# Attention scores from two fp32r products a head on stacked high and low parts, and in-chunk products over whole chunks

## The chip, the cores and the metric

The kernel runs on one core of one Trainium2 chip. The metric is the device time of one execution in microseconds. One execution was also profiled; its rows give the start and length of each instruction on five engines: PE (TensorE, the matrix engine; PEld are its weight loads), DVE (VectorE), ACT (ScalarE), POOL (GpSimd) and SP (SyncE, here only an issuer of transfers).

## The reference, cut to what matters

Two layers over 512 tokens of width 1024. The first mixes with a convolution and an RWKV-7 recurrence, the second with sliding-window attention; each is followed by a gated feed-forward block. The change touches two places: the products inside a chunk of the recurrence, which the kernel solves in chunks of 64 tokens, and the attention scores.

```python
def rwkv7_recurrence(r, w, k, v, a, b):
    def step(s, inp):
        r_t, w_t, k_t, v_t, a_t, b_t = inp
        sa = jnp.einsum('bhij,bhj->bhi', s, a_t)
        s = s * w_t[:, :, None, :] + sa[..., None] * b_t[:, :, None, :] + v_t[..., None] * k_t[:, :, None, :]
        return s, jnp.einsum('bhij,bhj->bhi', s, r_t)
...
    q = partial_rope(rms_norm(q, q_norm_g), positions)   # 16 heads of 64
    k = partial_rope(rms_norm(k, k_norm_g), positions)   # 4 heads of 64
...
    # blocks of 128 queries, each against its own and the block before
    s = jnp.einsum('bnqhgd,bnkhd->bnhgqk', q, kc).astype(jnp.float32) * (HEAD_DIM ** -0.5)
```

## The kernel before, in words

Activations lie with channels on the 128 partitions and the 512 tokens along the free dimension. Every large product goes through `gemm` (line 174): weights are loaded in pieces of 512 KB by SP, split into a high fp32r part on ACT (line 150) and a low remainder on DVE (line 151), and three fp32r matmuls of 128 rows and 512 columns (high by high, high by low, low by high) are added up in a PSUM bank. A tile framework orders the instructions of each engine ahead of time, by priorities and its own estimates; each engine then runs its list strictly in that order, and semaphores make it wait. Matmuls of `gemm` are therefore set between the small steps of the other work as filler, but at fixed places.

**In-chunk products** (`keys`, line 413). For each of four groups of channels (two heads each), each of 8 chunks and each head (`eo`), two products of 64 rows by 64 output rows by 128 columns in fp32 are formed, one for each half `d` of the output rows. They take the four 64 by 64 quarters of PE in turn. Four PSUM banks a group come from a ring of three, and DVE masks each bank into `mt` (line 415). The matmul of line 430 and, from the next group, that of line 372 follow.

**Attention.** `queries(j)` makes two query heads: a `gemm` of 24 matmuls, bias and gain on ACT (line 902), sums of squares on PE (line 900), and the rotation `rope`: POOL issues four small transfers that swap rows into `zr` (line 838), DVE multiplies by the signed sine (line 839), multiplies by the cosine and adds (lines 840, 841) into `qr`. Keys go through the same with a PE permutation (line 832) and are copied by eight POOL transfers into `kd`, which holds each of the four key heads twice, on partitions 0 to 63 and 64 to 127. `block(m, b)` then works on the four query heads of key head `m` and query block `b`: four fp32 matmuls on 64 rows give the scores (line 934; head `e` of a pair uses rows `e*64` on), DVE scales, masks and takes the row limit (line 939), ACT exponentiates (line 101), DVE normalizes (line 949), PE transposes (line 953), ACT copies (line 955), PE multiplies by the values on 64 output columns (line 960), and the result is split into `oh` and `ol` on ACT and DVE for the output `gemm`. In block 0 of a head only 128 keys are used, else 256. The loop calls `queries` for the next key head at `b` 0 and 2.

The forms in the profile's rows give the shape in which PE is used, rows by columns: 128\*128 for `gemm`, 64\*128 for the scores, 128\*64 for the product with the values, 128\*32 for the sums of squares, 64\*64 for the in-chunk products.

Of the kernel before, what the change touches and what calls it, by code (L numbers as in the profile page):

```python
# [11 lines left out]
F32 = mybir.dt.float32  # L12
F32R = mybir.dt.float32r
I32 = mybir.dt.int32
AF = mybir.ActivationFunctionType
ALU = mybir.AluOpType
# [3 lines left out]
P = 128  # L20
T = 512
# [8 lines left out]
L = 64  # L30
NCH = T // L
# [5 lines left out]
NKV = 4  # L37
HD = 64
# [7 lines left out]
T3 = 5  # L46
# [22 lines left out]
class Net:  # L69
# [186 lines left out]
    def mixer(self):  # L256
        nc, tc, ap = self.nc, self.tc, self.ap
        V, S, G = nc.vector, nc.scalar, nc.gpsimd
# [5 lines left out]
        with ExitStack() as es:  # L264
            pool = lambda **k: es.enter_context(tc.tile_pool(**k))
            self.banks(es, "m", "s", m=3, s=3, n=2)
            cst = pool(name="mxc", bufs=1)
            big = pool(name="mxb", bufs=1)
            tr = pool(name="mxt", bufs=2)
# [38 lines left out]
            msk = cst.tile([P, 1, P], F32, name="msk")  # L308
            G.memset(msk, 1.0)
            for h in range(2):  # L310
                hp = slice(h * L, (h + 1) * L)
# [52 lines left out]
            def keys(fc):  # L364
# [26 lines left out]
                bk = bks[fc] = t4([P, NCH, P], "bk")  # L391
                ar = tr.tile([P, NCH, P], F32, tag="ar", name="ar")
# [12 lines left out]
                mt = mts[g][:, i]  # L405

                for c0 in range(0, NCH, 4):
                    p4s = [self.psum().rearrange("p (c t) -> p c t", t=P) for _ in range(2)]
                    for c in range(4):
                        for d in range(2):  # L410
                            for eo in range(2):
                                hp, dp = slice(eo * 64, eo * 64 + 64), slice(d * L, (d + 1) * L)
                                nc.tensor.matmul(p4s[eo][dp, c, :], lhsT=bk[hp, c0 + c, dp], rhs=ar[hp, c0 + c, :], start=True, stop=True)
                    for eo in range(2):
                        V.tensor_tensor(out=mt[:, eo, c0 : c0 + 4, :], in0=p4s[eo], in1=msk.to_broadcast([P, 4, P]), op=ALU.mult)
                for d in range(2):
# [390 lines left out]
    def attention(self):  # L807
# [10 lines left out]
        with ExitStack() as es:  # L818
# [9 lines left out]
            def rope(dst, z, j=None):  # L828
                t = tq("rp")
                if j is None:  # L830
                    pp = self.bank("d")
                    nc.tensor.matmul(pp, lhsT=self.perm, rhs=z, start=True, stop=True)
                    V.tensor_tensor(out=t, in0=pp, in1=sin, op=ALU.mult)
                else:
                    pp = zr[j % 2]
                    for o in (0, 8, HD, HD + 8):
                        i = o ^ 8
                        G.dma_start(pp[o : o + 8, :], z[i : i + 8, :])
                    V.tensor_tensor(out=t, in0=pp, in1=self.sgs, op=ALU.mult)
                V.tensor_tensor(out=dst, in0=z, in1=cos, op=ALU.mult)  # L840
                V.tensor_tensor(out=dst, in0=dst, in1=t, op=ALU.add)


            kd = [cst.tile([P, T], F32, name=f"kd{m}") for m in range(NKV)]
            pk = self.gemm(wq, 8, xh, xl)
# [10 lines left out]
            for i in range(2):  # L856
                t = tq("zt")
                V.tensor_tensor(out=t, in0=pk[i], in1=rstd, op=ALU.mult)
                S.activation(out=t, in_=t, func=AF.Identity, bias=self.pc("attn_b_qkv", 8 + i))
                sq = tq("zs")  # L860
                S.activation(out=sq, in_=t, func=AF.Square)
                pss = self.bank("d")
                nc.tensor.matmul(pss, lhsT=self.bdv, rhs=sq, start=True, stop=True)
                rs = self.rsqrt_rows(tr, "t2", pss, 1e-6, "kr", ln=True)
                V.scalar_tensor_tensor(out=t, in0=t, scalar=self.pc("attn_k_norm_g"), in1=rs, op0=ALU.mult, op1=ALU.mult)
                kr = tq("kr")
                rope(kr, t)
                for e in range(2):
                    for o in range(2):
                        G.dma_start(kd[2 * i + e][o * HD : (o + 1) * HD, :], kr[e * HD : (e + 1) * HD, :])  # L870

# [14 lines left out]

            qr = cst.tile([P, 8, T], F32, name="qr")
            rq = cst.tile([P, NB, NH], F32, name="rq")

            def queries(j):  # L890
# [14 lines left out]
                V.tensor_scalar(out=ms, in0=pss, scalar1=1.0 / HD, scalar2=1e-6, op0=ALU.mult, op1=ALU.add)  # L905
                rope(qr[:, j, :], t, j)
                y0 = tr.tile([P, NB, 2], F32, tag="my", name="my")
# [6 lines left out]

            cst.tile([P, 112], F32, name="gap")
            oh = cst.tile([P, DC, T], F32R, name="oh")
            ol = cst.tile([P, DC, T], F32R, name="ol")

            def block(m, b):
# [10 lines left out]
                for hp in range(2):  # L930
                    for e in range(2):
                        h = 4 * m + 2 * hp + e
                        hs = slice(e * HD, (e + 1) * HD)
                        nc.tensor.matmul(pscs[e][:, hp, :nk], lhsT=qr[hs, h // 2, bs], rhs=kd[m][hs, k0 : k0 + nk], start=True, stop=True)  # L934
                for hp in range(2):
# [30 lines left out]
            for m in range(NKV):  # L966
                for b in range(NB):
                    if m < NKV - 1 and b % 2 == 0:
                        queries(2 * m + 2 + b // 2)
                    block(m, b)  # L970
# [77 lines left out]
```

## Time and profile before

| | us |
|---|---|
| median of 3 runs (lowest, highest) | 1225.57 (1220.81, 1232.14) |
| the profiled execution | 1226.35 |
| its span, first to last instruction | 1224.5 |
| PE busy in the span | 1202.0 |
| DVE, ACT, POOL busy in the span | 723.1, 553.0, 71.8 |

The span and what lies around it (1.85 us) make up the profiled execution's time. Busy PE time counts matmuls from start to modelled end, which overlap, so the step from one start to the next tells more than the mean length. Each fp32 matmul of the program is two instructions in the profile, except the transposes; an fp32r matmul is one.

### The profile page before, as it was taken

How to read it: one execution, taken by the hardware profiler on the slowest of the kernel's cores; microseconds unless marked ns; L12 is line 12 of the kernel's file. 1: busy time of each engine (PE TensorE's matmuls, PEld its weight loads, DVE VectorE, ACT ScalarE, POOL GpSimd, SP SyncE). 2: the span in 40 equal slices, each digit the busy share in tenths (PEclk: the TensorE clock that was granted, in tenths of full speed). 3: DMA queues.
4: the chain of work that ended last, by engine and by line, in shares of the span. 5: the costliest groups of instructions: out<-in, count | busy, mean ns of one | idle time of the engine just before them, and what ended most of it. 6: DMA issues, size and time to landing. Idle time of an engine off the chain costs nothing.

```text
span 1224.5 us, 17211 instructions
## 1 busy us (share of the span) xinstructions
PE 1202.0 (98%) x6547; PEld 945.2 (77%) x6547; DVE 723.1 (59%) x1366; ACT 553.0 (45%) x1035; POOL 71.8 (6%) x209
## 2 busy tenths in 40 slices
PE   7999999999999999999999999999999999999998
PEld 5677866568788888888888866668888888888886
DVE  6787974476767555553333778876655555553332
ACT  6877332375544434343222556774544344442221
POOL 4101031000100000000000031100000000000000
PEclk9999996999999999999999999999999999999999
DMA  5144391023322323223333231112223232233331
GB/s 190 50 115 117 94 219 34 2 70 104 99 90 100 104 86 104 98 91 96 98 103 100 87 93 56 42 36 86 88 101 102 87 104 95 95 104 103 120 113 60
DMA packets 65089, 114.45 MB, mean 93 GB/s; under 512 B 15680, under 2 KB 17936, under 8 KB 65008
## 3 DMA queue, kind: packets, MB, share of 16 engines
q1 hardware_dynamic: 60048, 102.25, 26.7%
q0 software_dynamic: 4816, 10.89, 3.6%
q8 instruction: 51, 0.84, 0.3%
q14 instruction: 30, 0.25, 0.1%
q10 hardware_dynamic: 144, 0.23, 0.1%
HBM read 105.40 MB, written 4.26 MB: 90 GB/s over the span
## 4 chain that ended last, share of the span: by engine, by line
PE 89%; DVE 6%; ACT 2%; issue 1%; DMA 1%; POOL 0%; ACTq 0%; DVEq 0%
PE mm L174 63%; PE bank L174 10%; PE mm L636 2%; PE bank L934 2%; PE bank L960 1%; PE bank L953 1%; DVE wlo L151 1%; PE ps L546 1%; PE ps L559 1%; PE ps L565 1%; DVE tb L494 1%; DVE etmp L492 1%; PE ps L530 1%; PE ps L523 1%; PE ps L573 1%
## 5 line engine op out<-in xcount | busy, mean ns | idle before, releaser
L151 DVE TENSOR_TENSOR wlo<-wraw,whi 128x512 fp32r<-128x512 f32 x364 | 250.7, 690 | 349.9 <-ACT whi L150 349.5
L150 ACT CAST whi<-wraw 128x512 fp32r<-128x512 f32 x364 | 225.1, 619 | 419.1 <-PE mm L174 380.5
L174 PE MATMUL mm<-xgh,whi 128*128 128x512 f32 x896 | 352.0, 393 | 9.3 <-ACT whi L150 7.8
L174 PE MATMUL mm<-xgl,whi 128*128 128x512 f32 x896 | 351.3, 392 | 0.0
L174 PE MATMUL mm<-xgh,wlo 128*128 128x512 f32 x896 | 350.8, 392 | 0.0
L174 PEld LDWEIGHTS mm<-xgh,whi 128*128 128x128 f32 x896 | 168.9, 189 | 46.0 <-ACT whi L150 9.2
L174 PEld LDWEIGHTS mm<-xgh,wlo 128*128 128x128 f32 x896 | 168.8, 188 | 38.1 <-issue 2.4
L174 PEld LDWEIGHTS mm<-xgl,whi 128*128 128x128 f32 x896 | 169.0, 189 | 36.3 <-issue 1.7
L174 PE MATMUL mm<-hh,wlo 128*128 128x512 f32 x352 | 137.0, 389 | 0.0
L174 PE MATMUL mm<-hh,whi 128*128 128x512 f32 x352 | 137.0, 389 | 0.0
L174 PE MATMUL mm<-hl,whi 128*128 128x512 f32 x352 | 137.0, 389 | 0.0
L174 PEld LDWEIGHTS mm<-hl,whi 128*128 128x128 f32 x352 | 66.1, 188 | 13.7
L174 PEld LDWEIGHTS mm<-hh,wlo 128*128 128x128 f32 x352 | 66.1, 188 | 13.7
L174 PEld LDWEIGHTS mm<-hh,whi 128*128 128x128 f32 x352 | 66.1, 188 | 13.7
L723 DVE SCALAR_TENSOR_TENSOR t<-gp,col,t 128x512 f32<-128x512 f32 x88 | 63.5, 745 | 0.0
L720 ACT ACTIVATE t<-gp,col 128x512 f32<-128x512 f32 x44 | 35.7, 816 | 35.3 <-DVE gp L718 34.7
L183 ACT CAST hh<-t 128x512 fp32r<-128x512 f32 x44 | 27.2, 621 | 37.0 <-DVE t L726 36.8
L718 DVE TENSOR_TENSOR gp<-mm,rstd 128x512 f32<-128x512 f32 x44 | 30.2, 691 | 17.3 <-PE mm L174 17.2
L726 DVE TENSOR_TENSOR t<-t,mm 128x512 f32<-128x512 f32 x44 | 30.0, 687 | 17.2 <-PE mm L174 17.2
L101 ACT ACTIVATE t<-t 128x512 f32<-128x512 f32 x44 | 27.7, 629 | 20.4 <-DVE t L723 20.3
L717 POOL MEMSET gp<- 128x2 f32 x44 | 4.4, 103 | 506.3 <-DVE t L723 451.0
L939 DVE CUSTOM_DVE_ANT_0 pr<-bank,mask,nsnk 128x256 f32<-128x256 f32 (+1 forms) x64 | 31.4, 503 | 2.0 <-PE bank L934 2.0
(328 smaller groups left out, 1442.8 us busy)
## 6 DMA issues: line engine op xcount, KB each, us to landing
wraw<-in_w_up_dram SPq DMA_DIRECT2D x88, 512.0 KB, 3.4
wraw<-in_w_down_dram SPq DMA_DIRECT2D x40, 512.0 KB, 3.6
wraw<-in_w_in_dram SPq DMA_DIRECT2D x22, 512.0 KB, 3.6
wraw<-in_w_qkv_dram SPq DMA_DIRECT2D x12, 512.0 KB, 3.4
wraw<-in_w_out_dram SPq DMA_DIRECT2D x8, 512.0 KB, 3.6
wraw<-in_w_o_dram SPq DMA_DIRECT2D x8, 512.0 KB, 3.4
st<-cpad POOLq DMA_DIRECT2D x24, 135.0 KB, 4.1
xT<-in_xT_dram SPq DMA_DIRECT2D x4, 512.0 KB, 7.9
```

The source lines that it names most:

```text
L101: ins = self.nc.scalar.activation(**kw)
L150: nc.scalar.copy(hi, src)
L151: nc.vector.tensor_tensor(out=lo, in0=src, in1=hi.bitcast(F32), op=ALU.subtract)
L174: mm = lambda a, b, **kw: self.nc.tensor.matmul(ps, lhsT=a[:, i, k, :], rhs=b[:, kk, :], **kw)
L183: nc.scalar.copy(hi, src)
L636: nc.tensor.matmul(pc[b * 32 : b * 32 + 32, :], lhsT=dg[:, b, g, :], rhs=stk[b][:, 4 * g : 4 * g + T], start=g == 0, stop=g == 7, tile_pos ...
L718: V.tensor_tensor(out=gp[:, 2:], in0=pg[i], in1=rstd, op=ALU.mult)
L720: S.activation(out=t, in_=gp[:, 2:], func=AF.Identity, scale=self.pc("ffn_conv_w", (3 * l + 2) * FC + f), bias=self.pc("ffn_conv_b", l * F ...
L723: V.scalar_tensor_tensor(out=t, in0=gp[:, j : j + T], scalar=self.pc("ffn_conv_w", (3 * l + j) * FC + f), in1=t, op0=ALU.mult, op1=ALU.add)
L726: V.tensor_tensor(out=t, in0=t, in1=pu[i], op=ALU.mult)
L934: nc.tensor.matmul(pscs[e][:, hp, :nk], lhsT=qr[hs, h // 2, bs], rhs=kd[m][hs, k0 : k0 + nk], start=True, stop=True)
L939: V.tensor_tensor_reduce(out=pr_[:, i, :nk], in0=pscs[e][:, hp, :nk], in1=mask[:, 2 * P - nk :], op0=ALU.add, op1=ALU.min, scale=rq[:, b, ...
```

## The change: what it does

In the recurrence, one product of 64 rows by 128 output rows by 128 columns takes the place of two, and the loop over the heads `eo` becomes the outer one: all 8 chunks of one head, then all of the other.

In attention, rotated queries and keys are split into a high fp32r part and a low remainder, each with a cast on ACT and a subtraction on DVE (`split`, lines 183 and 184). Keys: `kd` becomes 128 x 2 x 512, with the high part (index 0) and the low part (index 1) side by side, both on partitions 0 to 63 and again on 64 to 127. Queries: POOL transfers put, for head `e` of a pair, the high part on partitions `e*64` on and the low part on the other 64. The scores of a head are then two fp32r matmuls added up in the same bank: index 0 on all 128 rows (high and low queries by high keys), index 1 on the 64 rows of the high queries (by low keys). Both always run over 256 keys. The sine product of the queries' `rope` moves from DVE to POOL, its tiles move to the ring `t2`, `queries` are called at `b` 0 and 1, and 32 more POOL transfers are issued.

```diff
-                for c0 in range(0, NCH, 4):
-                    p4s = [self.psum().rearrange("p (c t) -> p c t", t=P) for _ in range(2)]
-                    for c in range(4):
-                        for d in range(2):
-                            for eo in range(2):
-                                hp, dp = slice(eo * 64, eo * 64 + 64), slice(d * L, (d + 1) * L)
-                                nc.tensor.matmul(p4s[eo][dp, c, :], lhsT=bk[hp, c0 + c, dp], rhs=ar[hp, c0 + c, :], start=True, stop=True)
-                    for eo in range(2):
-                        V.tensor_tensor(out=mt[:, eo, c0 : c0 + 4, :], in0=p4s[eo], in1=msk.to_broadcast([P, 4, P]), op=ALU.mult)
+                for eo in range(2):
+                    hp = slice(eo * 64, eo * 64 + 64)
+                    for c0 in range(0, NCH, 4):
+                        p4 = self.psum().rearrange("p (c t) -> p c t", t=P)
+                        for c in range(4):
+                            nc.tensor.matmul(p4[:, c, :], lhsT=bk[hp, c0 + c, :], rhs=ar[hp, c0 + c, :], start=True, stop=True)
+                        V.tensor_tensor(out=mt[:, eo, c0 : c0 + 4, :], in0=p4, in1=msk.to_broadcast([P, 4, P]), op=ALU.mult)
...
-                    V.tensor_tensor(out=t, in0=pp, in1=self.sgs, op=ALU.mult)
+                    G.tensor_tensor(out=t, in0=pp, in1=self.sgs, op=ALU.mult)
...
-            kd = [cst.tile([P, T], F32, name=f"kd{m}") for m in range(NKV)]
+            kd = [cst.tile([P, 2, T], F32R, name=f"kd{m}") for m in range(NKV)]
+            pair = lambda n: tr.tile([P, 2, 2, T], F32R, tag="qs", name=n, bufs=2)
+            ks = pair("ks")
...
+                self.split(ks[:, i, 0, :], ks[:, i, 1, :], kr)
                 for e in range(2):
                     for o in range(2):
-                        G.dma_start(kd[2 * i + e][o * HD : (o + 1) * HD, :], kr[e * HD : (e + 1) * HD, :])
+                        G.dma_start(kd[2 * i + e][o * HD : (o + 1) * HD], ks[e * HD : (e + 1) * HD, i])
...
-                rope(qr[:, j, :], t, j)
+                qr = t2("qr")
+                rope(qr, t, j)
+
+                if j % 2 == 0:
+                    qs[j // 2] = pair("qs")
+                q = [tr.tile([P, T], F32R, tag="t2", name=n, bufs=T3) for n in ("qh", "ql")]
+                self.split(q[0], q[1], qr)
+                for e in range(2):
+                    for d in range(2):
+                        G.dma_start(qs[j // 2][d * HD : (d + 1) * HD, j % 2, e, :], q[d ^ e][e * HD : (e + 1) * HD, :])
...
                 for hp in range(2):
-                    for e in range(2):
-                        h = 4 * m + 2 * hp + e
-                        hs = slice(e * HD, (e + 1) * HD)
-                        nc.tensor.matmul(pscs[e][:, hp, :nk], lhsT=qr[hs, h // 2, bs], rhs=kd[m][hs, k0 : k0 + nk], start=True, stop=True)
+                    for j in range(2):
+                        for e in range(2):
+                            hs = slice(e * HD, (e + 1) * HD) if j else slice(0, P)
+                            nc.tensor.matmul(pscs[e][:, hp, :], lhsT=qs[m][hs, hp, e, bs], rhs=kd[m][hs, j, k0 : k0 + 2 * P], start=j == 0, stop=j == 1)
...
-                    if m < NKV - 1 and b % 2 == 0:
-                        queries(2 * m + 2 + b // 2)
+                    if m < NKV - 1 and b < 2:
+                        queries(2 * m + 2 + b)
```

The order of PE's matmuls moves with it, at three places. The rows below are those of the built programs; one row may stand for several equal matmuls in a row (x4), numbers behind a name tell buffers apart, and L944, L963, L970 and L411 are the new lines of scores, transposes, products with the values and in-chunk products.

First, PE in the attention of the last key head (kd3), before:

```order
L953 MATMUL bank_7049<-ident_66,pr_7026 128x128 x4
L934 MATMUL bank_7110<-kd3_5653,qr_5955 128x256 x2
L953 MATMUL bank_7055<-ident_66,pr_7026 128x128 x4
L960 MATMUL bank_7061<-pT_7023,vt_5830 64x256 x2
L934 MATMUL bank_7154<-kd3_5653,qr_5955 128x256 x2
L960 MATMUL bank_7061<-pT_7023,vt_5830 64x256 x2
L934 MATMUL bank_7155<-kd3_5653,qr_5955 128x256 x2
L934 MATMUL bank_7199<-kd3_5653,qr_5955 128x256 x2
```

Now:

```order
L944 MATMUL bank_7227<-kd3_5590,qs_6846 128x256 x4
L174 MATMUL bank_7321<-ol_5900,whi_7359 128x512
L174 MATMUL bank_7321<-oh_5899,wlo_7360 128x512
L174 MATMUL bank_7321<-oh_5899,whi_7359 128x512
L174 MATMUL bank_7321<-ol_5900,whi_7359 128x512
L174 MATMUL bank_7321<-oh_5899,wlo_7360 128x512
L174 MATMUL bank_7322<-ol_5900,whi_7359 128x512
L944 MATMUL bank_7228<-kd3_5590,qs_6846 128x256 x4
L174 MATMUL bank_7322<-oh_5899,wlo_7360 128x512
L944 MATMUL bank_7276<-kd3_5590,qs_6846 128x256 x4
```

Two matmuls on 64 rows filled a bank's two heads before; now four do, for each of the two heads one on 128 rows and then one on 64, so the shape changes from one matmul to the next. Counted along the whole order from the first key rotation (line 832, now 829) to the end, PE's shape changes 101 times before and 176 times now; 136 of the 176 have a score matmul on one side or both (79 on both), against 58 before. From the first score matmul to the last product with the values stand 157 matmuls of `gemm` before and 120 now; the other 37 moved ahead of the first score.

Second, PE at the in-chunk products of the first group of channels, before:

```order
L174 MATMUL mm<-xgh,whi 128x512
L174 MATMUL mm<-xgl,whi 128x512
L413 MATMUL ps<-ar,bk 64x128 x24
L430 MATMUL bank<-rk,bd_191 128x512
L413 MATMUL ps<-ar,bk 64x128 x8
L372 MATMUL bank<-ku,bdh 128x512
L174 MATMUL mm<-xgh,wlo 128x512
```

Now:

```order
L174 MATMUL mm<-xgh,whi 128x512
L174 MATMUL mm<-xgl,whi 128x512
L411 MATMUL ps<-ar,bk 128x128 x16
L427 MATMUL bank<-rk,bd_191 128x512
L372 MATMUL bank<-ku,bdh 128x512
L174 MATMUL mm<-xgh,wlo 128x512
```

The second visit to the products behind line 430 is gone; the 16 wide ones stand together, 8 on the lower 64 rows and then 8 on the upper 64.

Third, PE at the end of attention, from the last transposes but one block on, before:

```order
L953 MATMUL bank<-ident,pr 128x128 x4
L174 MATMUL bank<-oh,whi 128x512
L174 MATMUL bank<-ol,whi 128x512
L960 MATMUL bank<-pT,vt 64x256 x2
L174 MATMUL bank<-oh,wlo 128x512
L960 MATMUL bank<-pT,vt 64x256 x2
L174 MATMUL bank<-oh,whi 128x512
L174 MATMUL bank<-ol,whi 128x512
L174 MATMUL bank<-oh,wlo 128x512
```

Now, from the last score matmuls on:

```order
L944 MATMUL bank<-kd_5590,qs 128x256 x3
L963 MATMUL bank<-ident,pr 128x128 x8
L970 MATMUL bank<-pT,vt 64x256 x4
L963 MATMUL bank<-ident,pr 128x128 x8
L970 MATMUL bank<-pT,vt 64x256 x4
L963 MATMUL bank<-ident,pr 128x128 x8
L970 MATMUL bank<-pT,vt 64x256 x4
L174 MATMUL bank<-oh,whi 128x512
```

The matmuls of the output `gemm` that stood between transposes and products with the values have moved ahead; none stands behind the last score until the last product.

## Rows read from the trace of the kernel before

**Rows 1.** The page: each engine's busy time.

```profile
PE 1202.0 (98%) x6547; PEld 945.2 (77%) x6547; DVE 723.1 (59%) x1366; ACT 553.0 (45%) x1035; POOL 71.8 (6%) x209
```

**Rows 2.** PE's waits, 690 to 835 us: for whom, total us, times, longest.

```profile
PE bank L953 <- DVE pr L949: 0.8, 2, 0.5
PE bank L960 <- ACT pT L955: 0.2, 1, 0.2
```

**Rows 3.** Two stretches: us, busy PE, PEld, DVE, ACT, POOL, clock, DMA, GB/s.

```profile
745.00:770.00 25.00, 25.00 (x196) 16.17 (x194) 21.28 (x83) 18.53 (x56) 4.01 (x8) 1.00 0.22 69
800.90:824.10 23.20, 22.82 (x135) 13.55 (x134) 17.56 (x75) 18.16 (x55) 0.00 (x0) 1.00 0.08 24
```

**Rows 4.** PE in order of time (start, us): fp32r on two shapes in turn.

```profile
32.81 0.39 PE L174 MATMUL mm<-xgh,wlo 128*128 128x512 f32 x1
33.04 0.39 PE L174 MATMUL mm<-xgh,whi 128*128 128x512 f32 x1
33.36 0.50 PE L359 MATMUL bank<-lis,lws 64*128 64x512 f32 x2
33.79 0.51 PE L174 MATMUL mm<-xgl,whi 128*128 128x512 f32 x1
34.22 0.73 PE L359 MATMUL bank<-lis,lws 64*128 64x512 f32 x4
```

**Rows 5.** PE in order of time: scores, last transposes, `gemm` again.

```profile
722.88 0.39 PE L174 MATMUL bank<-xgh,whi 128*128 128x512 f32 x1
723.40 0.92 PE L934 MATMUL bank<-kd,qr 64*128 64x128 f32 x6
...
747.07 1.13 PE L934 MATMUL bank<-kd,qr 64*128 64x256 f32 x4
748.13 1.09 PE L953 MATMUL bank<-ident,pr 128*128 128x128 f32 x8
748.98 0.47 PE L174 MATMUL bank<-xgh,wlo 128*128 128x512 f32 x1
...
812.03 1.13 PE L934 MATMUL bank<-kd,qr 64*128 64x256 f32 x4
...
821.30 0.27 PE L953 MATMUL bank<-ident,pr 128*128 128x128 f32 x1
...
824.11 0.50 PE L174 MATMUL bank<-oh,whi 128*128 128x512 f32 x1
```

**Rows 6.** PE in order of time: fp32r matmuls of 256 columns, one after the other.

```profile
701.63 0.28 PE L879 MATMUL mm<-wlo,xgh 128*128 128x256 f32 x1
701.75 0.28 PE L879 MATMUL mm<-whi,xgl 128*128 128x256 f32 x1
```

**Rows 7.** PE in order of time, without `gemm`: in-chunk products of the second group.

```profile
73.75 1.97 PE L413 MATMUL ps<-ar,bk 64*64 64x128 f32 x48 [0.15 <-DVE bk L395]
75.65 1.13 PE L430 MATMUL bank<-rk,bd 128*128 128x512 f32 x2
76.78 1.09 PE L413 MATMUL ps<-ar,bk 64*64 64x128 f32 x16
77.80 1.12 PE L372 MATMUL bank<-ku,bdh 128*128 128x512 f32 x2
```

**Rows 8.** POOL: two row swaps, landing times of `kd`, a selection, a fill.

```profile
716.31 1.02 POOL L838 DMA_DIRECT2D zr<-zt  x2
DMA to landing us min/median/max: 2.2/2.8/5.8
L313 POOL TENSOR_SCALAR_AFFINE_SELECT msk<-msk 64x64 f32<-64x64 f32 x4 | 2.6, 663 | 0.1
L826 POOL MEMSET zr<- 128x512 f32 x2 | 1.0, 528 | 148.3 <-DVE t L732 148.3
```

**Rows 9.** Groups by line, 690 to 835 us: a cast, a subtraction.

```profile
L151 DVE TENSOR_TENSOR wlo<-wraw,whi 128x512 fp32r<-128x512 f32 x26 | 17.7, 685 | 8.2 <-ACT whi L150 7.9
L150 ACT CAST whi<-wraw 128x512 fp32r<-128x512 f32 x26 | 16.0, 617 | 14.6 <-PE bank L174 12.3 <-PE mm L879 2.3
```

More of the change, by code (lines that the diff above doesn't have):

```diff
@@ L828, in rope @@
             def rope(dst, z, j=None):
-                t = tq("rp")
+                t = t2("rp")
                 if j is None:
@@ L838, in rope @@
                         G.dma_start(pp[o : o + 8, :], z[i : i + 8, :])
-                    V.tensor_tensor(out=t, in0=pp, in1=self.sgs, op=ALU.mult)
+                    G.tensor_tensor(out=t, in0=pp, in1=self.sgs, op=ALU.mult)
                 V.tensor_tensor(out=dst, in0=z, in1=cos, op=ALU.mult)
                 V.tensor_tensor(out=dst, in0=dst, in1=t, op=ALU.add)
-            kd = [cst.tile([P, T], F32, name=f"kd{m}") for m in range(NKV)]
+            cst.tile([P, 56], F32, name="gap0")
+            kd = [cst.tile([P, 2, T], F32R, name=f"kd{m}") for m in range(NKV)]
+            pair = lambda n: tr.tile([P, 2, 2, T], F32R, tag="qs", name=n, bufs=2)
+            ks = pair("ks")
             pk = self.gemm(wq, 8, xh, xl)
@@ L865, in attention @@
                 V.scalar_tensor_tensor(out=t, in0=t, scalar=self.pc("attn_k_norm_g"), in1=rs, op0=ALU.mult, op1=ALU.mult)
-                kr = tq("kr")
+                kr = t2("kr")
                 rope(kr, t)
+                self.split(ks[:, i, 0, :], ks[:, i, 1, :], kr)
                 for e in range(2):
                     for o in range(2):
-                        G.dma_start(kd[2 * i + e][o * HD : (o + 1) * HD, :], kr[e * HD : (e + 1) * HD, :])
+                        G.dma_start(kd[2 * i + e][o * HD : (o + 1) * HD], ks[e * HD : (e + 1) * HD, i])
             vt = cst.tile([P, NB, KD], F32, name="vt")
@@ L884, in attention @@
                 V.scalar_tensor_tensor(out=vt[:, b, :], in0=pvs[b][:, :KD], scalar=rt[:, b : b + 1], in1=self.bvr, op0=ALU.mult, op1=ALU.add)
-            qr = cst.tile([P, 8, T], F32, name="qr")
+            qs = {}
             rq = cst.tile([P, NB, NH], F32, name="rq")
@@ L913, in queries @@
                 V.tensor_tensor(out=rq[:, :, 2 * j : 2 * j + 2], in0=ms, in1=y0, op=ALU.mult)
-            cst.tile([P, 112], F32, name="gap")
+            cst.tile([P, 56], F32, name="gap")
             oh = cst.tile([P, DC, T], F32R, name="oh")
```

## The prediction

> **What bounds the kernel now.** I read the page first. PE is busy for 98% of the span [rows 1]: time is won or lost where PE's list of matmuls gets shorter or longer, or where PE is made to wait. Next I looked at the stage of the change, the attention from 702 to 824 us. PE waits there for about 1 us in all [rows 2]; it is busy for 25.00 of 25.00 us in its middle, while DVE is busy for 21.28 and ACT for 18.53 [rows 3]. So PE's own work sets the pace of this stage, with DVE some 15% behind it. Busy PE time says little about what a matmul costs, since neighbours overlap; I price matmuls by the step from one start to the next, in the listing of PE by time [rows 4 to 7].
>
> **The price of a change of shape.** In a run of `gemm` the next matmul starts 0.23 us after the last (32.81 and 33.04 in [rows 4]). Where PE goes from 128\*128 to 64\*128 and back, with fp32r on both sides, the steps are longer. The two matmuls of line 359 work on different halves of the rows, so together they need the time of one; their step to the next `gemm` matmul is 0.43 us, and the single `gemm` matmul that stands alone before the next pair also takes 0.43 (33.36, 33.79, 34.22 in [rows 4]). Each is 0.23 us plus 0.20 us, so a change of shape costs 0.20 us, each way. The fp32 scores show the same: two heads on the same rows, 256 columns, take 1.06 us up to the transposes (747.07 and 748.13 in [rows 5]), four instructions of 0.213 us and one change.
>
> The page TensorEngine Tiling (Array Packing) of the Trainium skill, section Tiling Modes, states that changing the tiling mode drains TensorE, while changing only the tile does not. That speaks against this change; the trace agrees, with 0.20 us for a drain. By the rule the sum below stands; without it, it would be 15.0 us lower.
>
> **Scores.** *Removed:* the 29 groups of score matmuls, from 723.40 to 812.03, take 25.3 us counted from each group's start to the next start of any other matmul (the first and the last are in [rows 5]). Each ends in one change of shape, so 29 x 0.20 = 5.8 us of that is switching and 19.5 us columns. *Added:* 64 heads, each with one fp32r matmul of 256 columns on 128 rows and one on 64. Such a matmul steps by 0.12 us [rows 6], so 128 x 0.12 = 15.4 us, less 0.5 us for the four places where two on different row halves stand together: 14.9 us. Columns gain 4.6 us. Block 0 of each key head, which used 128 keys, now pays for 256; this is in the count. *Switches:* the order changes shape 101 times before and 176 times now, 75 more, and 75 x 0.20 = 15.0 us. Scores therefore cost 15.0 - 4.6 = **+10.4 us** of PE.
>
> A check that the method closes: between 722.88 and 824.11 [rows 5], 157 `gemm` matmuls at 0.227, 112 transposes at 0.107 (eight from 748.13 to 748.98, 0.85 us), 28 pairs of value products at 0.43 (two output halves side by side, each with two instructions of 256 columns, like a score), about 1 us of line 900, 19.5 us of scores and 101 switches make 35.6 + 11.9 + 12.0 + 1.0 + 19.5 + 20.2 = 100.2 us. The trace has 101.2 us, of which about 1 us is waits.
>
> **In-chunk products.** Before, from the first product of a group to line 372, 77.80 - 73.75 = 4.05 us [rows 7]; the four groups take 4.15, 4.05, 4.05 and 4.00. All four quarters of PE work at once at first, then two. Now 8 products on the lower rows and 8 on the upper stand in a row: each is two fp32 instructions of 128 columns at 0.107 us, and only at the border do two row halves overlap, so 15.5 x 0.213 = 3.3 us. With one switch (0.2) and line 430's matmul, which needs four times the 0.213 of its 128-column kin, 0.85 us, that is 4.35 us, 0.3 us more a group: **+1.2 us**. The second visit with its two switches, which the change saves, is in this. Bounds: 0 if the row halves overlap more than the order shows, +3 if the fourth bank waits for DVE to mask the first.
>
> **DVE, ACT, POOL.** Eight query splits and two key splits put ten casts of 0.62 us on ACT and ten subtractions of 0.69 us on DVE [rows 9]; eight sine products of the same 128x512 shape leave DVE. DVE gains about 1.4 us of work and ACT 6.2 us, over 100 us in which they have 15% and 25% to spare: nothing on the path by itself, and up to 7.6 us if all cover were gone. POOL takes the eight sine products. No POOL arithmetic on 128x512 is in this trace; the nearest rows are a fill of that size, 0.53 us, and a selection on an eighth of its columns, 0.66 us, so up to 5.3 [rows 8]. I take 1.6 us, three times the fill (two reads and a write against one write), since the fill has the right size. Behind a sine product on POOL's list wait the next pair's row swaps and the 32 new transfers, about 0.52 us each to issue.
>
> The first scores depend on this chain: swaps issued by 717.3 [rows 8], landed 2.8 us later at the row's median, 720.1; sine product 1.6, multiply and add 1.4, split 1.3, four issues 2.1, landing 2.8: 729.3 us. The order sends 37 more `gemm` matmuls ahead of the first score, which moves it from 723.4 to 723.4 + 37 x 0.227 = 731.8. Covered, so 0, up to 2 us if the sine product takes 5.3 or landing the row's maximum of 5.8. The wider `kd` transfers land earlier than the queries and cost nothing.
>
> **The end of attention.** What was filler there is gone. After the last score PE now has 2 x (0.85 + 0.85 + 0.4) = 4.2 us of other products before the last block's transposes. Before, these came at 821.30, 8.2 us after the last scores, which start at 812.03 and take 1.06 [rows 5], in a stretch where ACT was busy for 18.16 and DVE for 17.56 of 23.20 us [rows 3]. If that chain still takes 8.2 us, PE waits 4.0; if it is only the shortest path (reduce, exponent, denominator, normalize, about 4.3 us), nothing. I take half, 2.0, and 0.5 for the value products that now wait for ACT's copies as the last one does [rows 2]: **+2.5 us**, between 0 and 6.
>
> **Sum.** 10.4 + 1.2 + 2.5 = 14.1 us on the profiled execution's 1226.35 (span 1224.5 and 1.85 around it): 1240.5. The median of the runs lies 0.8 us lower, so I say 1240. Bounds: all low, 10.4 + 0, 1236; all high, 10.4 + 3 + 6 + 2, 1247.
>
> **Rivals.**
> *Switching inside a head's sum is free.* The 79 changes of shape between two score matmuls might cost nothing: both are fp32r, and the second continues the first's sum in the same bank. Then 79 x 0.20 = 15.8 us falls away: 1240.5 - 15.8 = 1225, no slower than before. For it: no row shows such a pair in one bank. Against it: rows 4 show fp32r to fp32r at the full price. It decides if such a switch costs under 0.02 us.
> *Half the price.* If a switch behind a short matmul of 256 columns costs 0.10, those 79 cost 7.9 less: 1232.
> *DVE and ACT become the bound.* Without filler among the blocks, PE meets their chains directly, and every us added to either shows. With the 7.6 us above exposed as well: 1248. Against it: their spare time [rows 3]. GPSIMD Engine Reference of the Trainium skill, section 1 (Specifications), adds that POOL shares its memory interfaces with VectorE and contends with VectorE instructions that read two tensors; no row here has the two together.
>
> **How the numbers follow.** Forecast 0.60, free switching 0.12, half price 0.12, DVE and ACT 0.16. The range takes the forecast's bounds, half price and a part of the third rival, 1228 to 1249; free switching and times above are left out. About 1% (12 us) is what this measurement can tell from no change; that lies at 1238. Slower by over 1%: most of the forecast (0.42 of 0.60) and the third rival, 0.57. Within 1%: the rest of the forecast, half price and most of free switching, 0.39. Faster by over 1%: 0.04.
>
> **What would show it.** Right: in the attention, PE steps of about 0.32 us from every score matmul to the next of the other shape; the stage from the first key rotation to the last value product some 13 us longer; in-chunk groups of about 4.35 us; idle PE before the last transposes. Wrong: steps of 0.12 us between the two products of a head; or long waits of PE on DVE, ACT or a transfer amid the blocks.

## The result, and the profile after

| | median of the runs, us (lowest, highest) | profiled execution | span | granted clock, mean of the span |
|---|---|---|---|---|
| before | 1224.05 (1220.81, 1232.14; 4 runs) | 1226.35 | 1224.5 | 0.988 |
| after | 1269.65 (1262.53, 1274.69; 4 runs) | 1273.56 | 1271.8 | 0.964 |

The ratio is 1.036, with an interval of 1.030 to 1.041: slower by 46 us. The forecast of 1240 and its range, which ended at 1249, were both too low; the direction was right.

The page of the changed kernel is no help at first. PE is busy for 97% of a longer span, with fewer instructions than before [rows 1]:

```profile
PE 1240.0 (97%) x6419; PEld 966.5 (76%) x6419; DVE 730.5 (57%) x1368; ACT 559.8 (44%) x1045; POOL 99.1 (8%) x249
```

What differs is the row of the granted TensorE clock, in tenths, 40 slices of the span. First the page before, then the page after:

```profile
PEclk9999996999999999999999999999999999999999
```
```profile
PEclk9999999999999999999999965969999999999999
```

The dip of before in the seventh slice (184 to 214 us) no longer shows, and deeper ones stand in the 24th, 25th and 27th slice, in the attention. The stretches of the changed kernel there, in the columns of [rows 3] (the clock is third from the end):

```profile
728.00:740.00 12.00, 12.00 (x77) 8.05 (x76) 6.24 (x24) 6.35 (x21) 5.86 (x10) 1.00 0.35 92
741.00:787.00 46.00, 44.51 (x183) 25.53 (x183) 23.52 (x97) 19.85 (x64) 10.78 (x18) 0.50 0.12 27
787.00:805.00 18.00, 15.16 (x65) 8.76 (x63) 12.82 (x41) 8.77 (x26) 5.51 (x9) 0.78 0.47 117
805.00:831.00 26.00, 26.00 (x185) 17.45 (x183) 19.49 (x74) 17.57 (x55) 8.81 (x14) 1.00 0.18 47
836.00:864.00 28.00, 25.92 (x76) 15.11 (x74) 11.12 (x53) 11.45 (x40) 1.03 (x2) 0.52 0.08 17
```

A granted clock of 0.50 is the lower of TensorE's two levels, 1.2 GHz instead of 2.4. From 741 to 787 us PE ran at it throughout, although it was busy for 44.51 of 46 us. Time lost to the clock, taken as (1 - clock) x length: 23.0 + 4.0 + 13.4 = 40.4 us in the three low stretches. That counts PE's idle time in them too (6.4 us, of which a faster clock would have saved nothing), so it is some 3 us too much. The blocks before stood at 1.00 in the two stretches of [rows 3]; between these, the trace of before has one short stretch at the lower level, with PE busy throughout:

```profile
737.00:741.00 4.00, 4.00 (x17) 2.80 (x17) 3.39 (x18) 0.85 (x3) 0.44 (x1) 0.57 0.06 12
```

PE by time in the changed kernel, at both levels (start, length). A row of scores names the shape of its first matmul only; inside it 128\*128 and 64\*128 alternate, two matmuls a head, so x8 is four heads, x4 two and x2 one:

```profile
728.83 1.22 PE L944 MATMUL bank<-kd,qs 128*128 128x256 f32 x4
729.98 0.50 PE L174 MATMUL bank<-xgh,wlo 128*128 128x512 f32 x1
...
736.48 1.83 PE L944 MATMUL bank<-kd,qs 128*128 128x256 f32 x6
738.24 0.51 PE L174 MATMUL bank<-xgl,whi 128*128 128x512 f32 x1
...
763.61 1.09 PE L944 MATMUL bank<-kd,qs 128*128 128x256 f32 x2
764.63 1.12 PE L970 MATMUL bank<-pT,vt 128*64 128x256 f32 x4
...
819.74 2.46 PE L944 MATMUL bank<-kd,qs 128*128 128x256 f32 x8
822.12 0.50 PE L174 MATMUL bank<-ol,whi 128*128 128x512 f32 x1
```

Two heads take 1.15 us up to the next matmul at full clock, three take 1.76, four 2.38. Each head more adds 0.61 to 0.62, two steps of 0.31 us. At half clock one head takes 1.02, two steps of 0.51. Nothing waits between 728 and 740 us, and from 736.48 on the list is scores on two shapes in turn with single `gemm` matmuls between them: there, at 740.3 us, the clock falls. The same run of scores brings it down without a wait in two versions below, attention alone (at 753 us) and the changed kernel with the queries first (at 745 us).

PE's waits, 690 to 875 us, in the columns of [rows 2]:

```profile
PE bank L970 <- ACT pT L965: 3.6, 5, 1.8
PE bank L944 <- DMA qs<-ql: 3.3, 2, 1.9
PE bank L963 <- DVE pr L959: 3.3, 3, 2.0
PE bank L944 <- DVE nm L949: 1.4, 2, 0.8
PE bank L963 <- DVE ol L184: 1.0, 2, 0.6
```

They are 13.5 us with two small ones more, where before they were 1.3 us. The transfers' 3.3 us are 1.44 us ahead of the first score (726.74 us) and 1.89 us before a score at 838.80. The second fall begins at 835.8 us, ahead of that wait and behind one of 2.0 us on DVE's `pr`, which ended at 835.37.

In the recurrence, PE by time, the group of [rows 7]:

```profile
73.22 3.47 PE L411 MATMUL ps<-ar,bk 64*128 64x128 f32 x32
76.62 1.12 PE L427 MATMUL bank<-rk,bd 128*128 128x512 f32 x2
77.58 1.02 PE L372 MATMUL bank<-ku,bdh 128*128 128x512 f32 x2
```

From the first product to line 372 that is 77.58 - 73.22 = 4.36 us (4.05 before). POOL's groups by line, whole span: the sine product, which had no row before, takes 1.30 us.

```profile
L836 POOL TENSOR_TENSOR rp<-zr,sgs 128x512 f32<-128x512 f32 x8 | 10.4, 1304 | 6.8 <-DMA zr<-zt 6.7
```

**Where the time went.** The profiled executions differ by 47.2 us. The first key rotation starts at 694.8 us instead of 702.3: 7.5 us gained in what lies ahead. From it to the start of the last value product it took 120.7 us (702.3 to 823.0) and takes 175.6 (694.8 to 870.4): 54.9 us lost. Summed in windows of 5 us from 690 to 900, (1 - clock) x length is 1.7 us before and 40.9 after, 39.2 us more. Counted whole, that leaves 15.7 of the 54.9 for shapes, columns and waits. But the count takes all time at the lower level as half lost, and a step of the scores takes 0.51 us there instead of 0.31, not twice as long. The runs on record give a rate, each with its own mean clock: within a kernel, a run takes 0.81 us longer for each us more of (1 - clock) x span (a line through 150 runs of the kernel before, the changed one and the twelve below). By that rate, an estimate, the clock's part of the 54.9 is 32 us and 23 are left. The prediction had 12.9 for these 23 (10.4 and 2.5) and nothing for the 32.

### The profile page after: what moved, and what is told of

The parts are those of the page before. It is cut to its first block, busy times and chain, and to the rows that moved or that the text cites. A ratio compares the mean times of both kernels' runs of the same rounds, so it can differ in the third digit from the quotient of the medians.

```text
span 1271.8 us, 17059 instructions
## 1 busy us (share of the span) xinstructions
PE 1240.0 (97%) x6419; PEld 966.5 (76%) x6419; DVE 730.5 (57%) x1368; ACT 559.8 (44%) x1045; POOL 99.1 (8%) x249
## 4 chain that ended last, share of the span: by engine, by line
PE 91%; ACT 3%; DVE 3%; DMA 2%; issue 1%; SPq 0%; POOL 0%; DVEq 0%; POOLq 0%
PE mm L174 65%; PE bank L174 10%; PE bank L944 3%; PE mm L633 2%; PE bank L970 2%; PE bank L963 1%; PE ps L411 1%; DMA xT<-in_xT_dram 1%; PE ps L543 1%; PE ps L562 1%; PE ps L556 1%; DMA qs<-ql 1%; DMA zr<-zt 0%; PE ps L570 0%; PE bank L359 0%
## 5 line engine op out<-in xcount | busy, mean ns | idle before, releaser
L944 PE MATMUL bank<-kd,qs 64*128 64x256 f32 (+1 forms) x128 | 51.7, 464 | 4.7 <-DMA qs<-ql 3.3
L944 PEld LDWEIGHTS bank<-kd,qs 64*128 64x128 f32 (+1 forms) x128 | 29.7, 240 | 32.4 <-issue 20.9
```

The lines of the kernel that those rows point to most:

```text
L944: nc.tensor.matmul(pscs[e][:, hp, :], lhsT=qs[m][hs, hp, e, bs], rhs=kd[m][hs, j, k0 : k0 + 2 * P], start=j == 0, stop=j == 1)
```

## The experiments

The theory to test: changes of shape thin out PE's work so far that the granted clock falls (A). Its rivals: waits on DVE, ACT and the transfers bring it down, with a `gemm` that the order moved ahead of the first score (B); or the in-chunk products do the harm (C). Changes of shape are counted along PE's order in the attention: 101 before, 176 after. Each ratio is to runs of the kernel before on the same chip, whose median lay between 1222.8 and 1226.7 us in all comparisons (the chip was not the same in all of them, so versions are best compared by their ratios).

**One part at a time: in-chunk products alone, attention alone.** The first is the kernel before with the part of the diff for `keys`, the second the changed kernel without it.

> The kernel before with the wide in-chunk products alone. Theory A: no loss here; 1226 us if the 7.5 us that the recurrence stage was shorter in the changed kernel's trace are chance, 1217 us if they come from the wide products. Rival B: the same. Rival C: 1265 us.

Measured: 1217.23 us (1216.67 to 1221.15), ratio 0.9945 (0.9926 to 0.9965).

> The changed kernel with the narrow in-chunk products of before. Theory A: the whole loss is here, 1265 to 1280 us, clock in the attention near 0.75. Rival B: the same. Rival C: 1226 us.

Measured: 1278.28 us (1274.97 to 1283.51), ratio 1.0455 (1.0403 to 1.0507). C is refuted: the wide products gain 7 us, the attention loses 54. (In the profiled execution of the attention alone, 6.4 of its 48.9 us lie ahead of the attention.) The gain, though each group takes 0.3 us more, comes from a later place. Windows of the kernel before around the dip in the seventh slice, and of this one:

```profile
165.00:180.00 15.00, 12.46 (x84) 5.84 (x82) 10.71 (x16) 4.13 (x5) 5.39 (x10) 1.00 1.14 212
180.00:195.00 15.00, 14.94 (x239) 12.25 (x240) 6.39 (x9) 4.08 (x7) 4.18 (x8) 0.53 0.34 85
```
```profile
165.00:180.00 15.00, 15.00 (x148) 8.75 (x147) 9.79 (x14) 4.54 (x6) 4.96 (x10) 1.00 0.98 210
180.00:195.00 15.00, 14.37 (x255) 9.98 (x252) 7.74 (x11) 5.71 (x10) 4.76 (x9) 0.83 0.50 119
```

Before, PE idled for 2.5 us of the first stretch (the longest wait, 2.2 us, of line 636 on DVE's `lt`) and then ran at 0.53; with the wide products the order has other matmuls there, PE does not idle, and the clock is 0.83. So the wait and much of the clock went together.

The kernels with the narrow products have a second weak place in the recurrence. Windows of the kernel before, and of a version with short products on 64 rows that comes below:

```profile
255.00:275.00 20.00, 18.22 (x164) 13.61 (x165) 15.27 (x29) 13.98 (x27) 0.93 (x1) 1.00 0.33 106
```
```profile
255.00:275.00 20.00, 19.38 (x133) 14.04 (x131) 11.46 (x22) 7.70 (x18) 0.93 (x1) 0.50 0.32 106
```

The clock was at 0.50 to 0.54 there in the profiled executions of four of the five kernels with the narrow products, and at 1.00 in those of all nine with the wide ones. So executions of one kernel differ by what the clock does, by some 10 us here, and a single profile does not stand for all of them.

**The same order of work, both products on 128 rows.** Only the rows of the second product change (the 64 more bring in the product of the two low parts, which the changed kernel leaves out). PE's order stays; 64 changes of shape are left of 176.

```diff
-                            hs = slice(e * HD, (e + 1) * HD) if j else slice(0, P)
+                            hs = slice(0, P)
```

> Both products of a head run on 128 rows (the second is then high and low queries by low keys); order, transfers and splits stay those of the changed kernel, and shape changes in the attention fall from 176 to 64. Theory A, the drains at shape changes thin out PE's work until the granted clock is halved: the clock in the attention stays above 0.95, and drains and clock both go, 1200 to 1218 us. Rival B, waits for POOL's transfers and for DVE and ACT halve the clock: the clock in the attention stays near 0.75 and only drains go (112 x 0.2 us, some of it at half clock), 1240 to 1252 us. Rival C, the in-chunk products made the loss: about 1265 us.

Measured: 1241.29 us (1239.82 to 1243.39), ratio 1.0141 (1.0106 to 1.0176). 28 us of the 46 go with 112 changes of shape. Neither theory had it as it came: the time lies in B's range, but B had the clock stay low, and its loss from 690 to 900 us fell from 40.9 to 17.1 us; A had no loss left, and what is left stands behind waits. PE by time, where the first fall begins:

```profile
738.69 0.74 PE L944 MATMUL bank<-kd,qs 128*128 128x256 f32 x4
740.90 0.50 PE L944 MATMUL bank<-kd,qs 128*128 128x256 f32 x2 [1.47 <-DVE nm L949]
742.60 0.47 PE L963 MATMUL bank<-ident,pr 128*128 128x128 f32 x1 [1.20 <-DVE pr L959]
```

**One fp32 product on 64 rows, from the high parts.** All transfers, splits and the order of `queries` stay as in the changed kernel, the low parts are left out of the scores; 107 changes of shape.

```diff
-                    for j in range(2):
...
+                        hs = slice(e * HD, (e + 1) * HD)
+                        nc.tensor.matmul(pscs[e][:, hp, :nk], lhsT=qs[m][hs, hp, e, bs].bitcast(F32), rhs=kd[m][hs, 0, k0 : k0 + nk].bitcast(F32), start=True, stop=True)
```

> The changed kernel, but a head's scores are one fp32 product of the high parts on 64 rows (the low parts are left out of the scores); splits, transfers and POOL's sine product stay, so the waits stay, and shape changes fall from 176 to 107, as before (101). Theory A: clock in the attention above 0.95, time 1222 to 1235 us. Rival B: clock near 0.75 there, 1250 us or more. Rival C: about 1265 us.

Measured: 1236.54 us (1227.59 to 1239.99), ratio 1.0078 (1.0045 to 1.0111). With nearly the changes of before there are waits of 6.5 us from 690 to 880 and 10.2 us of lost clock: 12 us more than before, although the wide in-chunk products, worth 7, are in it. So what the changed kernel adds beside the new scores (the longer chain for the queries, the `gemm` moved ahead) costs something by itself, and neither pure A nor pure B holds.

**Changes of shape alone.** The kernel before, with a product of 2 columns ahead of each of the 64 score products (the score product overwrites them). In one version it stands on 128 rows (167 changes), in the other on the 64 rows of the score that follows (104). The order of the work is the same in both; what differs is the rows of the short product, and with them 63 changes.

```diff
+                        nc.tensor.matmul(pscs[e][:, hp, 0:2], lhsT=xh[:, 0, bs], rhs=xh[:, 0, 0:2], start=True, stop=True)
```

> The kernel before, with one product of 2 columns on 128 rows ahead of each of the 64 score products (it writes two columns that the score product then overwrites). Nothing waits longer than before and the gemm stands where it stood, but TensorE changes its shape 167 times in the attention instead of 101. Theory A (draining for a change of shape is enough to bring the granted clock down): 66 x 0.20 = 13 us of changes and 64 x about 0.03 of columns make 1240 us at full clock, and the clock in the blocks falls besides, as it did in the changed kernel, by half or more of its 41 us: 1255 to 1280. Theory B (the clock falls only where waits and an early gemm leave the blocks thin; changes cost their 0.20 us and no more): 1236 to 1242, granted clock 1.00 from the first score to the last value product. Theory C (a change costs little by itself): 1226 to 1230.

> The same 64 short products in the same places, on the 64 rows of the score product that follows, so that shapes change 104 times in the attention (101 in the kernel before). All theories: 64 x 0.03 to 0.06 us of columns and start, 1224 to 1230, clock 1.00 in the blocks. What the run before gives above this one is the price of 63 changes of shape and of nothing else: theory A 25 to 50 us, theory B 12 to 15, theory C under 4.

Measured: on 128 rows 1258.92 us (1252.87 to 1266.97), ratio 1.0248 (1.0170 to 1.0327); on 64 rows 1230.96 (1224.62 to 1242.01), ratio 1.0044 (1.0004 to 1.0084). So 63 changes of shape cost 28.0 us without a wait (some 11 us either way, by the two intervals). Not all of it is changes. On 64 rows, PE by time in that version:

```profile
739.94 0.28 PE L934 MATMUL bank<-xgh 64*128 64x2 f32 x2
740.08 0.69 PE L935 MATMUL bank<-kd,qr 64*128 64x256 f32 x4
...
741.24 0.69 PE L954 MATMUL bank<-ident,pr 128*128 128x128 f32 x4
```

Four heads on the two halves of the rows run in pairs here and take 1.30 us. With a product on 128 rows between them they run one after the other, at 0.83 us each (738.72 to 739.55 below). In all, 24 of the 128 score instructions start together with another in the version on 64 rows and 6 in the one on 128, which is worth 3.4 us of the 28.0 (4096 columns at 0.213 us for 256, an estimate); the rest is 0.39 us a change. Of the version on 128 rows, first all of PE's waits from 690 to 880 us, then PE by time where the clock falls, then the windows around it:

```profile
PE bank L954 <- DVE ol L184: 0.3, 1, 0.3
PE bank L961 <- ACT pT L956: 0.3, 1, 0.3
PE bank L832 <- DVE zt L865: 0.3, 1, 0.3
```
```profile
738.72 0.70 PE L935 MATMUL bank<-kd,qr 64*128 64x256 f32 x2
739.35 0.27 PE L932 MATMUL bank<-xgh 128*128 128x2 f32 x1
739.55 0.70 PE L935 MATMUL bank<-kd,qr 64*128 64x256 f32 x2
740.18 0.27 PE L932 MATMUL bank<-xgh 128*128 128x2 f32 x1
```
```profile
727.00:739.00 12.00, 12.00 (x85) 8.01 (x84) 9.86 (x36) 7.61 (x24) 1.97 (x4) 1.00 0.18 51
739.00:754.00 15.00, 15.00 (x83) 9.09 (x83) 7.33 (x32) 7.18 (x23) 1.97 (x4) 0.66 0.14 40
```

PE has scores and short products in turn from 737.80 us on, is never idle, and the clock falls from 1.00 to 0.66 over the next stretch. From 690 to 900 us the clock costs 17.0 us there and 5.1 us with all on 64 rows (counted whole, as all lost clock below). That 5.1 is one fall, from 760 to 771 us, in a profiled execution that took 1242.01 us, the longest of its ten. Ahead of it too stands a run of short matmuls on changing shapes, without a wait:

```profile
757.00:760.00 3.00, 3.00 (x45) 2.14 (x46) 2.17 (x8) 1.52 (x6) 1.50 (x4) 1.00 0.35 135
```

In these 3 us PE goes from products of line 900 (128\*32) to transposes and scores and back. Why such a run brought the clock down in some places and executions and not in others, no run shows.

**Half of them.** The short product on 128 rows ahead of the second pair of heads alone, on 64 rows ahead of the first: same order, 147 changes.

```diff
+                        sh = slice(0, P) if hp else slice(e * HD, (e + 1) * HD)
```

> The 64 short products in the same order as in both earlier versions with short products, now on 128 rows ahead of the second pair of heads of a block and on 64 rows ahead of the first: 147 changes of shape in the attention (104 with all on 64 rows, 167 with all on 128 rows). Of the 28.0 us between those two, drains at 0.20 us are 12.6 and lost clock the rest. If each change adds its share, 104 to 147 is 43 of 63 changes: 19 us, 1250 us. If there is a point from which the clock falls, the clock in the blocks either stays as with all on 64 rows (5 us lost; 43 x 0.20 = 8.6, 1240 us) or is as low as with all on 128 rows (17 us lost; 1252 to 1256).

Measured: 1243.78 us (1236.37 to 1248.49), ratio 1.0163 (1.0113 to 1.0213). The profiled execution lost 1.7 us of clock from 690 to 900. From the first key rotation to the last value product the three versions take 129.4, 134.2 and 151.5 us, less lost clock 124.3, 132.5 and 134.5: 8.2 us for 43 changes and 10.2 us for 63, or 0.19 and 0.16 each; 2.2 and 3.4 us of these are score instructions that no longer start together, which leaves 0.14 and 0.11. The profile is that of the reading in which the clock stays up, and the mean clock of the four runs, 0.979 to 0.993, lies where that of the ten with all on 64 rows lies (0.978 to 0.994; 0.970 to 0.981 on 128). By the ratios, however, 43 of the 63 changes take 0.58 of the whole difference, close to a share in proportion (0.68). The spread of the runs and one profile do not settle whether there is a point from which the clock falls.

**The queries' `gemm` ahead of the values'.** The block of code for the values moves behind `queries(1)`, once with both products on 128 rows (54 changes), once in the changed kernel (161).

```diff
-            pvs = [self.pmm() for _ in range(NB)]
...
             queries(0)
             queries(1)
+            vt = cst.tile([P, NB, KD], F32, name="vt")
+            pvs = [self.pmm() for _ in range(NB)]
```

> Both products of a head on 128 rows (54 changes of shape in the attention), and the first two queries' gemm ahead of the values' gemm instead of behind it: 52 matmuls of the queries' gemm stand ahead of the first score (110 in the changed kernel and in the version with both products on 128 rows alone, 73 in the kernel before) and 128 among the blocks (118; 155 before). Theory A (drains alone lower the clock): 54 changes are few, no fall, 1205 to 1222, and no more than the 17 us of lost clock below the 1241 of the version without the move. Theory B (waits for the queries' chain and an early gemm make the blocks thin and lower the clock): the waits on the transfers go, the clock falls less, 1215 to 1232. If waits on DVE and ACT among the blocks cause it, neither moves: 1236 to 1245, clock falling at the same places.

> The changed kernel with the first two queries' gemm ahead of the values' gemm: 161 changes of shape (176), 52 matmuls of the queries' gemm ahead of the first score (110), 128 among the blocks (118). Theory A (drains): 161 changes still bring the clock down, 1255 to 1275. Theory B (waits and an early gemm): the first fall, which lasts 46 us at the lower level, goes, 1235 to 1252.

Measured: 1237.46 us (1235.61 to 1245.89), ratio 1.0105 (1.0074 to 1.0136), and 1263.45 us (1253.43 to 1267.75), ratio 1.0270 (1.0190 to 1.0349). They lie 3.8 and 6.2 us under their versions without the move, and the intervals overlap. The early `gemm` is not the main cause: with it set right, 161 changes still lose 29.0 us of clock, and 107 changes less take 26 us off. With 54 changes the time lies in the range that was given for waits on DVE and ACT, and 8.5 us of clock are still lost. The longest of PE's waits from 690 to 880 us, and two windows:

```profile
PE bank L948 <- DVE pr L944: 5.0, 9, 1.3
PE bank L929 <- DMA qs<-ql: 4.5, 2, 2.2
PE bank L929 <- DVE nm L934: 3.1, 4, 2.4
```
```profile
740.00:760.00 20.00, 17.14 (x87) 11.37 (x86) 17.50 (x63) 13.76 (x45) 5.57 (x9) 0.83 0.25 54
760.00:780.00 20.00, 16.59 (x154) 11.27 (x152) 18.62 (x68) 14.95 (x50) 9.78 (x16) 1.00 0.26 60
```

In the second, DVE is busy for 18.62 of 20 us and PE for 16.59: DVE is now the busier of the two, and PE waits for it.

**The stacking transfers on SP's queue**, with both products on 128 rows and the queries first (62 changes):

```diff
-                        G.dma_start(qs[j // 2][d * HD : (d + 1) * HD, j % 2, e, :], q[d ^ e][e * HD : (e + 1) * HD, :])
+                        nc.sync.dma_start(qs[j // 2][d * HD : (d + 1) * HD, j % 2, e, :].bitcast(F32), q[d ^ e][e * HD : (e + 1) * HD, :].bitcast(F32))
```

> Both products of a head on 128 rows, queries' gemm first, and the queries' 32 transfers to the stacked tile issued from SP's queue instead of POOL's, where 22.4 us of waits for the high part stood ahead of the sine rows' transfers and the sine product. If POOL's order makes TensorE wait (4.5 us on the transfers and part of the 8 us on DVE): those waits go, and with them clock; 1215 to 1230. If DVE's work sets the pace (78 to 93% busy from 740 to 800 in the version with POOL's queue): 1233 to 1242, waits on DVE as before. If SP's queue delays the weights behind the transfers: above 1240, with waits of ACT's conversion on the weights' DMA.

Measured: 1232.14 us (1229.06 to 1234.25), ratio 1.0070 (1.0046 to 1.0094). PE's waits on the transfers are gone, those on DVE stay at about their size:

```profile
PE bank L948 <- DVE pr L944: 3.7, 6, 1.9
PE bank L929 <- DVE nm L934: 3.2, 5, 2.3
```

The time fell by about what the transfers' waits had been; the two intervals overlap. That POOL's order has a part in the loss is thus likely and not shown; the waits on DVE are still there.

**The sine product back on DVE**, in the changed kernel (`V.tensor_tensor` for `G.tensor_tensor`):

> The changed kernel with the sine product of the queries back on DVE (0.69 us each there, 1.30 on POOL), so the edit to POOL alone is undone. If POOL's slower product and the queue behind it make the queries late, 2 to 5 us less, 1264 to 1268; if DVE is the tighter engine, 8 x 0.69 = 5.5 us of DVE more, of which PE sees at most that: 1270 to 1277. In neither case does the clock loss of 41 us in the blocks move by more than 10 us, since changes of shape stay at 173.

Measured: 1264.88 us (1257.23 to 1273.18), ratio 1.0321 (1.0270 to 1.0372), with 37.6 us of lost clock. That cannot be told from the changed kernel (1.0304 to 1.0411): the sine product on POOL is not the cause.

**The wide in-chunk products and the early queries, without the change to the scores:**

> The kernel before with the wide in-chunk products and the first two queries' gemm ahead of the values' gemm, scores as before: 96 changes of shape in the attention (101), none of the queries' gemm between values and first score, 180 of its matmuls among the blocks (155). It tells what the earlier queries are worth without the change to the scores. If the gemm among the blocks is what keeps the granted clock up and TensorE free of waits: clock 1.00 from first score to last value product, 5 x 0.20 = 1 us of changes less, 1214 to 1219, at or a little under the 1217 of the wide products alone. If DVE and ACT fall behind once scores start earlier: waits on them of 3 to 8 us among the blocks, 1219 to 1228.

Measured: 1218.46 us (1216.77 to 1221.10), ratio 0.9956 (0.9929 to 0.9983); PE waits about 2 us from 690 to 830, clock 1.00 throughout. It is as fast as the wide products alone. Those two versions are some 0.5% faster than the kernel before; none with the new scores is.

## Why the prediction was wrong

**The step that failed** is the sum, which took every term at the full clock. "10.4 + 1.2 + 2.5" has no term for the clock, though the prediction showed PE's 1.00 of before [rows 3] and counted that 75 changes of shape would be added. [rows 3] left out the stretch of before from 737 to 741 us at 0.57, the one sign in that trace that the attention's clock can fall. The runs put in its place: 63 changes added cost 28.0 us, where 0.20 us each makes 12.6; 3.4 are scores that no longer run side by side, and 11.9 us more of lost clock were counted in the trace, while PE's list had no waits. In the changed kernel the lower level cost about 32 us of the 54.9. That the clock falls during scores on two shapes in turn is what four traces show; what exactly it needs was not measured.

The page TensorE: Matmul & The Clock Gate of the Trainium skill, section A second HAM failure mode: psum-queue depth-cycling, describes a kernel in which PE idles briefly between groups of matmuls, so often that its clock goes back and forth between the two levels. The traces here would agree if the drain between two shapes is such an idle time. The profile does not show it as one, since PE counts as busy for 15.00 of 15.00 us; so no run here shows that it is.

**The price of a change of shape** was right: a step from one score matmul to the next of the other shape takes 0.31 us in the changed kernel, 0.12 of it columns, so 0.19 for the change where 0.20 was said (the versions with short products leave 0.11 to 0.14). The prediction's sign of being right, steps of about 0.32 us, is there, so steps of 0.12, the rival of *free switching*, are refuted, and *half the price* too. The page TensorE: Matmul & The Clock Gate of the Trainium skill, section Single matmul latency, puts the time that the array needs to drain at about 175 ns. These rows are near it; that the two are the same time no run here shows.

**Scores** by that price: 75 x 0.19 - 4.6 = 9.7 us at full clock, for 10.4 predicted.

**DVE and ACT become the bound** was true in part, as a rival with 0.16, and is the second step that failed. In the changed kernel PE waits for them for 9.3 us. All waits are 13.5 us instead of 1.3: 12.2 more, where the sum had 2.5. With the 9.7 of the scores that makes 21.9, close to the 23 us that are left when the clock's part is taken off. When the changes of shape are taken out, the waits on DVE and ACT grow (14.1 us with both products on 128 rows, 6.3 of them on the normalized rows) and keep that kernel slower than before. The prediction let the added casts and subtractions hide beside PE's work and priced the loss of that cover at up to 7.6 us; it did not say that the clock falls behind such waits as well. Its own sign of being wrong, long waits amid the blocks, came: up to 2.0 us on DVE and 1.9 on a transfer.

**The first scores' chain** was said to be covered, 0 to 2 us: PE waited 1.44 us for the last transfer, within the bounds.

**The end of attention**, 2.5 us: from 859 us on PE waits 0.61, 1.77 and 0.35 us, 2.7 in all. Right in size, with luck: the 2.0 in it was taken as half of a range from 0 to 4.

**In-chunk products**: 4.36 us in the group of [rows 7] for 4.35 predicted. But the whole effect was -7 us, not +1.2: a wait and a stretch at the lower clock 100 us later went with the new order. Without this part the loss would have been 54 us instead of 46.

**DVE, ACT, POOL**: the sine product took 1.30 us, 1.6 was estimated; put back on DVE it changes nothing that can be measured.

## What to carry to other kernels

Where PE's granted clock stands at 1.00 and the change adds short matmuls on changing shapes or takes filler away, price that stage a second time at half clock, as the bad case: a change of shape, 0.19 us by its step and counted as busy by the profile, cost about 0.4 us with what the clock lost. Look for the places where the clock of before already fell; here one stood between the two stretches that were read. Read the clock's row of the page first when PE is "97% busy" and the time is longer. And test a change in parts: here one part gained 0.5% and the other lost 4.5%. Where one kernel's runs differ, look at the mean clock of each run before comparing two profiles.

## What the runs showed of the hardware that was not expected

The granted clock fell to its lower level while PE counted as busy without a gap (12.00 of 12.00 us up to 739, then 15.00 of 15.00 at 0.66), with nothing added to the kernel before but short matmuls on another shape; it came back to 1.00 from 805 to 831 us in the changed kernel, where runs of `gemm` matmuls stood between the scores. Within a kernel, a run took 0.81 us longer for each us of (1 - clock) x span. Two scores on different halves of the rows started together where nothing of another shape stood between them. A product of 2 columns in place was nearly free where its shape was that of its neighbour (64 of them: 1.0004 to 1.0084) and far from it where it was not (1.0170 to 1.0327). POOL multiplied two 128x512 fp32 tiles in 1.30 us, DVE subtracts such tiles in 0.69 [rows 9].
